# Moving the start of the MLP's operands by 216 bytes within their tiles, in a two-layer encoder on one core

## The chip, the cores and the metric

The kernel runs on one core of a Trainium2 chip. The metric is the device time of one execution in microseconds (us). The kernel before takes 2055.51 us, the median of three runs (2053.45 to 2055.89).

## What is computed

The reference is a two-layer bidirectional encoder in float32, with 256 tokens of width 2048. Each layer adds a token mixer with cross-attention, and then a dense MLP with squared ReLU of width 8192. The change concerns the MLP, so only its part is shown in full:

```python
h = x
for i in range(DEPTH):                       # 2 layers
    n = rms_norm(h, attn_norm[i])
    ...                                      # attention heads, concatenated
    h = h + jnp.concatenate([mix, cross], axis=-1) @ w_o[i]
    n = rms_norm(h, mlp_norm[i])
    h = h + jnp.square(jax.nn.relu(n @ w_up[i])) @ w_down[i]
return rms_norm(h, final_norm)
```

## The kernel before, in words

Every matrix product is done on float32 data split in two parts: ScalarE (ACT) copies a value into the rounded type float32r, the "hi" part (line 303), and VectorE (DVE) subtracts it from the value to leave the "lo" part (line 304). A product is then three matmuls: hi x hi, hi x lo and lo x hi. In a matmul one operand stays in the array (the weights in the trace's sense, loaded by an instruction of its own that the profile shows as PEld) and the other is moved past it.

**The MLP.** Its input, hT, holds the normalised activations by feature: 128 partitions, 16 blocks of 512 columns, the first 256 of a block being the hi part of the 256 tokens and the next 256 the lo part. It is a tile of tag "wide" in the pool "keep", got by `wide` (line 423), which gives 512 bytes of room and takes an offset in bytes, `at`. The attention's input nT uses the same tag at offset 480; hT uses 0 (line 617).

The up weights come in chunks of 128 x 2048, each in one DMA into the tile raw_U (`loaded`). `half_of_side` (line 706) splits half a chunk, 128 x 1024, into two tiles uh and ul, each with 256 bytes of room and two buffers; it has an offset in bytes too, `place`, which is 0 for the up products. Other callers give it MOVING_AT = 160: three chunks of the second layer's input projection that are prepared early (`prep_early`) and the last, plain part of the down product (`plain_grains`), where uh and ul are the moved operand.

`u_products` (line 696) does eight blocks of one half chunk, three matmuls each (lines 702, 703, 704): uh against the hi part of hT, uh against its lo part, and ul against the hi part. In all three the 128 x 128 slice of uh or ul is the weights and 256 columns of hT move. A chunk is 48 such matmuls, and the two layers have 128 chunks, 6144 matmuls in all. The result, ps_u, goes through ReLU and square on ACT (lines 756, 757).

The down product is done by a scheme that saves products: per step a set "first" (bh, bl; three products) and a set "second" (th, tl; four products), three matmuls of 512 columns for each product (lines 816, 817, 818). Here the activations a_s are the weights and the split down weights move. There are 112 such steps, and the last eighth of the hidden width goes through plain products (lines 208, 211, 212).

**Order.** The kernel lists "grains" of work (`add_mlp`): first the up products of the hidden width's first eighth, then alternately half a chunk of up products and one set of the down side, for seven eighths, then the plain part. Each grain has earlier stages for loading and splitting, called a fixed number of grains ahead. A scheduler then sets the order on each engine. On PE it comes out as 48 up matmuls, then 12 on th and tl, then 9 on bh and bl, and so on; in some steps two of the 48 stand ahead of the last down matmuls.

Of the kernel before, what the change touches and what calls it, by code (L numbers as in the profile page):

```python
# [40 lines left out]
GUARD = 3  # L41

MOVING_AT = 160
MASKED = -1e30


# [27 lines left out]
def encoder_kernel(ctx: ExitStack, tc: tile.TileContext, t: dict, out: bass.AP):  # L74
# [4 lines left out]
    def opened(name, side="left", space=None, bufs=1):  # L79
        kw = {"space": space} if space else {}  # L80
        manager = tc.tile_pool(name=name, bufs=bufs, side=side, reuse_waits="tile", **kw)
        pools[name] = manager, manager.__enter__()
        return pools[name][1]

    def closed(*names):
        for name in names:
            pools.pop(name)[0].__exit__(None, None, None)
# [56 lines left out]
    def halves_of(w):  # L144
# [6 lines left out]
        def prep_early(hf):  # L151
            tiles[hf] = half_of_side(tiles["raw"], hf, MOVING_AT)

# [35 lines left out]
    def later(n, fn, *args):  # L189
        pending.append((state["tick"] + n, fn, args))  # L190
# [110 lines left out]
    def split(dst_hi, dst_lo, src):  # L301

        first = nc.scalar.activation(dst_hi, src, AF.Copy)  # L303
        return first, nc.vector.tensor_tensor(dst_lo, src, dst_hi.bitcast(F32), op=ALU.subtract)  # L304
# [10 lines left out]
    def transposed(dst, src, ks, which):  # L315

        for a in range(0, len(ks), 2):
            pt = at.att.tile([P, 2, SEQ], F32, tag="att", name="pt_n")
            for b, k in enumerate(ks[a : a + 2]):
                for i in range(NT):  # L320
                    nc.tensor.transpose(pt[:, b, i * P : (i + 1) * P], src(i, k), ident)  # L321
            for b, k in enumerate(ks[a : a + 2]):
                last = split_pair(dst, pt[:, b, :], which, k)
        return last
# [98 lines left out]
    def wide(name, at=0):  # L423
        room = keep.tile([P, KT * 512 + P], F32R, tag="wide", name=name)
        return room[:, at // 4 : at // 4 + KT * 512].rearrange("p (a b) -> p a b", b=512)
# [164 lines left out]
    def sum_squares(which, i, nb):  # L590
        sq = at.side.tile([P, 512], BF16, tag="junk", bufs=1, name="sq")
        nc.scalar.activation(sq, h[:, i, nb * 512 : (nb + 1) * 512], AF.Square,
                             accum_out=ssq[which][:, i, nb : nb + 1])

    def mean_square(which, n, name):

        s = small.tile([P, NT], F32, tag="ss0", name="ss_t")
        nc.vector.tensor_reduce(s, ssq[which][:, :, :n], axis=AX.X, op=ALU.add)
        v = keep.tile([P, NT], F32, tag=name, name=name)
        nc.vector.tensor_scalar(v, s, 1.0 / (n * 512), EPS, op0=ALU.mult, op1=ALU.add)  # L600
        return v
# [7 lines left out]
    def o_done(layer, nb):  # L609
        which = 2 * layer  # L610

        def guard():

            box["near"] = mean_square(which, GUARD, "near")
            box["scale"] = keep.tile([P, NT], F32, tag="scale", name="scale")
            nc.gpsimd.tensor_tensor(box["scale"], box["near"], mhalf[:, :NT], op=ALU.pow)
            box["hT"] = wide(f"hT{layer}")

        def begun():

            y = at.side.tile([P, NT, 512], F32, tag="T", bufs=2, name="h_s")
            for i in range(NT):
                nc.scalar.activation(y[:, i, :], h[:, i, D - 512 :], AF.Copy, scale=box["scale"][:, i : i + 1])
            box["begun"] = y

        def scaled(b):
            y = at.side.tile([P, NT, 512], F32, tag="T", bufs=2, name="h_s")
            for i in range(NT):
                nc.scalar.activation(y[:, i, :], h[:, i, b * 512 : (b + 1) * 512], AF.Copy,
                                     scale=box["scale"][:, i : i + 1])  # L630
            transposed(box["hT"], lambda i, k: y[:, i, k % 4 * P : (k % 4 + 1) * P],
                       list(range(b * 4, b * 4 + 4)), (G_M0, G_M1)[layer])

        def inv():

            v = mean_square(which, 4, "full")
            box["inv"] = keep.tile([P, NT], F32, tag="inv", name="inv")
            nc.vector.reciprocal(v, v)
            nc.vector.tensor_tensor(box["inv"], v, box["near"], op=ALU.mult)
            box["ninv"] = keep.tile([P, NT], F32, tag="ninv", name="ninv")  # L640
            nc.vector.tensor_scalar(box["ninv"], box["inv"], -1.0, None, op0=ALU.mult)

        def f(w):
            if nb == 0:
                closed("work")
                at.side = opened("side", side="right")
            def add():
                for i in range(NT):
                    hs = h[:, i, nb * 512 : (nb + 1) * 512]
                    nc.vector.tensor_tensor(hs, w.ps[i], hs, op=ALU.add)  # L650

            def squares():
                for i in range(NT):
                    sum_squares(which, i, nb)

            if nb < 3:
                add()
                squares()
            if nb == GUARD - 1:
                later(1, guard)  # L660
                for b in range(GUARD):
                    later(2 + 2 * b, scaled, b)
                later(7, begun)
            if nb == 3:
                y = box["begun"]
                for i in range(NT):
                    nc.vector.scalar_tensor_tensor(y[:, i, :], w.ps[i], box["scale"][:, i : i + 1], y[:, i, :],
                                                   op0=ALU.mult, op1=ALU.add)
                box["ready"] = transposed(box["hT"], lambda i, k: y[:, i, k % 4 * P : (k % 4 + 1) * P],
                                          list(range(12, KT)), (G_M0, G_M1)[layer])  # L670
                later(4, past, add)
                later(6, past, squares)
                later(8, past, inv)
        return f
# [28 lines left out]
            nc.tensor.matmul(ps, hi[:, s], acts[:, k, SEQ:], start=False, stop=False)  # L703
            nc.tensor.matmul(ps, lo[:, s], acts[:, k, :SEQ], start=False, stop=k == KT - 1)  # L704

    def half_of_side(raw, hf, place=0):
        s = slice(place // 4, place // 4 + HALF)
        tiles = tuple(at.side.tile([P, HALF + 64], F32R, tag=n, bufs=2, name=n)[:, s] for n in ("uh", "ul"))
        box.setdefault("splits", []).append(split(*tiles, raw[:, hf * HALF : (hf + 1) * HALF]))
        return tiles  # L710
# [6 lines left out]
    def up_grains(layer, part, m):  # L717
# [5 lines left out]
        def prep(hf):  # L723
            own[hf] = half_of_side(own["raw"], hf)
# [145 lines left out]
    def plain_grains(layer, nb):  # L870
# [9 lines left out]
        def prep(c, hf):  # L880
            if c == 0:
                own[c, hf] = half_of_side(own[0], hf, MOVING_AT)
            else:
                own[c, hf] = tuple(at.mlp.tile([P, HALF], F32R, tag="bt"[hf] + x, name=f"{x}_p") for x in "hl")
                split(*own[c, hf], own[1][:, hf * HALF : (hf + 1) * HALF])
# [273 lines left out]
def expanded_bias(rpb):  # L1159
# [6 lines left out]
    dc = np.clip(cols[None, :] - cols[:, None] + WIN_W - 1, 0, 2 * WIN_W - 2)  # L1166
    res = np.full((nh, 2, GRID_W, BJ, GRID_W), MASKED, np.float32)
    for r in range(2):
        for j in range(BJ):
            dr = j + ROWS + 1 - r  # L1170
            res[:, r, :, j, :] = np.where(inside[None], rpb[:, dr][:, dc], np.float32(MASKED))
    return res.reshape(nh, P, BJ * GRID_W)
# [64 lines left out]
```

## Time and profile before

| | |
|---|---|
| median of three runs | 2055.51 us |
| the profiled execution | 2053.93 us |
| its span, first to last instruction | 2052.1 us |
| granted TensorE clock, mean | 0.999 |
| PE busy | 2029.9 us, 12516 matmuls |
| up products (lines 702, 703, 704), 2048 matmuls each | 568.6, 567.9 and 568.4 us busy, 278 ns each |
| split of uh (ACT, line 303) | 278 of 1061 ns |
| split of ul (DVE, line 304) | 278 of 1219 ns |

Matmuls are pipelined: one of 256 columns is shown with 278 ns, yet the next one starts some 113 ns after it. So for PE the rows' durations and the busy share don't tell the rate; the differences between start times in the timeline do. In the timeline a row gives the start in us from the span's start, the duration in us, engine, line, operation, the tiles (result <- moved operand and weights) and the shapes. A table of stretches gives, for each engine, busy time and in brackets the number of instructions that began there.

### The profile page before, as it was taken

How to read it: one execution, taken by the hardware profiler on the slowest of the kernel's cores; microseconds unless marked ns; L12 is line 12 of the kernel's file. 1: busy time of each engine (PE TensorE's matmuls, PEld its weight loads, DVE VectorE, ACT ScalarE, POOL GpSimd, SP SyncE). 2: the span in 40 equal slices, each digit the busy share in tenths (PEclk: the TensorE clock that was granted, in tenths of full speed). 3: DMA queues.
4: the chain of work that ended last, by engine and by line, in shares of the span. 5: the costliest groups of instructions: out<-in, count | busy, mean ns of one | idle time of the engine just before them, and what ended most of it. 6: DMA issues, size and time to landing. Idle time of an engine off the chain costs nothing.

```text
span 2052.1 us, 31583 instructions
## 1 busy us (share of the span) xinstructions
PE 2029.9 (99%) x12516; PEld 1812.2 (88%) x12516; DVE 1669.2 (81%) x2061; ACT 1252.7 (61%) x1652; POOL 119.3 (6%) x144
## 2 busy tenths in 40 slices
PE   8999999999999999999999999999999999999998
PEld 7888888889999999999988888889999999999996
DVE  6767666558998999989897667657988999999896
ACT  6755555556666666666656557556666666666664
POOL 0000000000000000000000001000000000000000
PEclk9999999999999999999999999999999999999999
DMA  7755555727777777787765554536877787887773
GB/s 280 283 190 179 188 176 171 276 88 223 231 231 231 221 237 230 220 243 224 225 218 205 176 180 144 194 116 221 242 226 231 217 238 221 237 229 224 235 219 135
DMA packets 93429, 433.79 MB, mean 211 GB/s; under 512 B 10464, under 2 KB 12128, under 8 KB 60128
## 3 DMA queue, kind: packets, MB, share of 16 engines
q1 hardware_dynamic: 75888, 399.25, 57.7%
q0 software_dynamic: 16816, 31.46, 8.7%
q8 instruction: 98, 1.61, 0.3%
q10 hardware_dynamic: 576, 1.05, 0.1%
q14 instruction: 51, 0.42, 0.1%
HBM read 398.17 MB, written 4.19 MB: 196 GB/s over the span
## 4 chain that ended last, share of the span: by engine, by line
PE 97%; ACT 1%; DVE 1%; issue 0%; DMA 0%; SPq 0%; POOLq 0%; POOL 0%; ACTq 0%
PE ps_u L704 11%; PE ps_u L702 11%; PE ps_u L703 11%; PE p L816 9%; PE p L817 9%; PE p L818 9%; PE ps_m L208 8%; PE ps_m L211 8%; PE ps_m L212 8%; PE ps_s L221 6%; PE ps_s L224 3%; PE pt_a L384 1%; PE pt_n L321 1%; DMA raw<-in_w_km 0%; PE av L392 0%
## 5 line engine op out<-in xcount | busy, mean ns | idle before, releaser
L704 PE MATMUL ps_u<-hT,ul 128*128 128x256 f32 x2048 | 568.4, 278 | 1.8 <-DVE ul L304 1.8
L702 PE MATMUL ps_u<-hT,uh 128*128 128x256 f32 x2048 | 568.6, 278 | 0.2
L703 PE MATMUL ps_u<-hT,uh 128*128 128x256 f32 x2048 | 567.9, 277 | 0.0
L303 ACT ACTIVATE uh<-raw_U 128x1024 fp32r<-128x1024 f32 x278 | 294.8, 1061 | 315.8 <-PE ps_u L703 294.8
L304 DVE TENSOR_TENSOR lo<-raw,hi 128x1024 fp32r<-128x1024 f32 (+1 forms) x224 | 266.4, 1195 | 161.7 <-ACT hi L303 158.4
L702 PEld LDWEIGHTS ps_u<-hT,uh 128*128 128x128 f32 x2048 | 384.9, 188 | 5.8 <-ACT uh L303 0.6
L704 PEld LDWEIGHTS ps_u<-hT,ul 128*128 128x128 f32 x2048 | 385.9, 189 | 3.7 <-DVE ul L304 2.6
L703 PEld LDWEIGHTS ps_u<-hT,uh 128*128 128x128 f32 x2048 | 384.4, 188 | 4.5
L304 DVE TENSOR_TENSOR ul<-raw_U,uh 128x1024 fp32r<-128x1024 f32 x278 | 337.6, 1219 | 40.5 <-ACT uh L303 40.4
L303 ACT ACTIVATE hi<-raw 128x1024 fp32r<-128x1024 f32 (+1 forms) x224 | 231.7, 1039 | 210.4 <-PE ps_m L212 117.8
L303 ACT ACTIVATE th<-t 128x2048 fp32r<-128x2048 f32 x112 | 215.1, 1920 | 123.5 <-PE p L818 117.1
L304 DVE TENSOR_TENSOR tl<-t,th 128x2048 fp32r<-128x2048 f32 x112 | 256.3, 2288 | 34.5 <-ACT th L303 34.1
L304 DVE TENSOR_TENSOR bl<-b,bh 128x1536 fp32r<-128x1536 f32 x112 | 196.1, 1751 | 0.3 <-ACT bh L303 0.2
L817 PE MATMUL p<-tl,a_s 128*128 128x512 f32 x448 | 177.2, 395 | 0.0
L818 PE MATMUL p<-th,a_s 128*128 128x512 f32 x448 | 174.4, 389 | 0.0
L303 ACT ACTIVATE bh<-b 128x1536 fp32r<-128x1536 f32 x112 | 166.2, 1484 | 10.2 <-PE p L818 4.0
L816 PE MATMUL p<-th,a_s 128*128 128x512 f32 x448 | 166.1, 395 | 0.0
L796 POOL DMA_DIRECT2D t<-b x112 | 97.1, 867 | 1164.5 <-DVE t L795 510.3
L221 PE MATMUL ps_s<-nT,hi 128*128 128x512 f32 x448 | 142.5, 397 | 0.0
L818 PE MATMUL p<-bh,a_s 128*128 128x512 f32 x336 | 131.1, 390 | 0.0
L817 PE MATMUL p<-bl,a_s 128*128 128x512 f32 x336 | 130.9, 390 | 0.0
L795 DVE TENSOR_TENSOR t<-t,b 128x512 f32<-128x512 f32 x112 | 77.2, 689 | 50.8 <-DMA t<-in_w_pair 43.7
(237 smaller groups left out, 3508.2 us busy)
## 6 DMA issues: line engine op xcount, KB each, us to landing
raw_U<-in_w_up SPq DMA_DIRECT2D x128, 1024.0 KB, 6.6
b<-in_w_pair SPq DMA_DIRECT2D x112, 768.0 KB, 4.5
raw<-in_w_o SPq DMA_DIRECT2D x32, 1024.0 KB, 5.0
t<-in_w_pair SPq DMA_DIRECT2D x112, 256.0 KB, 3.4
t<-b POOLq DMA_DIRECT2D x112, 256.0 KB, 6.7
raw<-in_w_b SPq DMA_DIRECT2D x21, 1024.0 KB, 4.9
raw<-in_w_av SPq DMA_DIRECT2D x12, 1024.0 KB, 4.9
raw<-in_w_aq SPq DMA_DIRECT2D x12, 1024.0 KB, 4.9
```

The lines of the kernel that those rows point to most:

```text
L208: first = nc.tensor.matmul(w.ps[i], ah, hi[:, s], start=st, stop=False)
L211: nc.tensor.matmul(w.ps[i], ah, lo[:, s], start=False, stop=False)
L212: nc.tensor.matmul(w.ps[i], al, hi[:, s], start=False, stop=sp)
L221: nc.tensor.matmul(ps, hi[:, s], acts[:, k0 + j, :], start=k0 + j == 0, stop=False)
L303: first = nc.scalar.activation(dst_hi, src, AF.Copy)
L304: return first, nc.vector.tensor_tensor(dst_lo, src, dst_hi.bitcast(F32), op=ALU.subtract)
L702: nc.tensor.matmul(ps, hi[:, s], acts[:, k, :SEQ], start=k == 0, stop=False)
L703: nc.tensor.matmul(ps, hi[:, s], acts[:, k, SEQ:], start=False, stop=False)
L704: nc.tensor.matmul(ps, lo[:, s], acts[:, k, :SEQ], start=False, stop=k == KT - 1)
L816: nc.tensor.matmul(ps, a[:, 0, ai, :], hi[:, s], start=begins, stop=False)
L817: nc.tensor.matmul(ps, a[:, 0, ai, :], lo[:, s], start=False, stop=False)
L818: nc.tensor.matmul(ps, a[:, 1, ai, :], hi[:, s], start=False, stop=ends)
```

## The change

hT begins 216 bytes further on in its tile, and so do uh and ul wherever no other offset is given, that is in the up products. 216 bytes are 54 float32 elements. The tiles keep their sizes and their places, since the room was there already; the calls with MOVING_AT = 160 and nT at 480 stay.

```diff
 MOVING_AT = 160
+UP_AT = 216
 MASKED = -1e30
...
             nc.gpsimd.tensor_tensor(box["scale"], box["near"], mhalf[:, :NT], op=ALU.pow)
-            box["hT"] = wide(f"hT{layer}")
+            box["hT"] = wide(f"hT{layer}", UP_AT)
...
-    def half_of_side(raw, hf, place=0):
+    def half_of_side(raw, hf, place=UP_AT):
         s = slice(place // 4, place // 4 + HALF)
         tiles = tuple(at.side.tile([P, HALF + 64], F32R, tag=n, bufs=2, name=n)[:, s] for n in ("uh", "ul"))
```

## The prediction

> **What bounds the kernel now.** I read the page's busy line first, then the chain that ended last.
>
> ```profile
> PE 2029.9 (99%) x12516; PEld 1812.2 (88%) x12516; DVE 1669.2 (81%) x2061; ACT 1252.7 (61%) x1652; POOL 119.3 (6%) x144
> ...
> PE 97%; ACT 1%; DVE 1%; issue 0%; DMA 0%; SPq 0%; POOLq 0%; POOL 0%; ACTq 0%
> ```
>
> TensorE is busy for 99% of the span and makes up 97% of the chain. So a matmul that starts a nanosecond later after its predecessor moves the end by a nanosecond; nothing else matters much. The table of stretches says the same of one inner eighth of an MLP (eight steps of 10.31 us), and gives two stretches of the eighth's opening, when up products run alone, in layer 0 (from 462 us) and layer 1 (from 1390 us):
>
> ```profile
> core 0: us, PE busy (x) PEld busy (x) DVE busy (x) ACT busy (x) POOL busy (x), PEclk, DMA share, GB/s
> ...
> 584.50:667.00 82.50, 82.50 (x554) 75.47 (x553) 74.56 (x80) 54.54 (x57) 6.98 (x8) 1.00 0.78 231
> 462.00:482.00 20.00, 20.00 (x179) 20.00 (x178) 13.42 (x16) 12.42 (x18) 1.05 (x1) 1.00 0.58 179
> 1390.00:1410.00 20.00, 20.00 (x172) 20.00 (x171) 12.28 (x15) 11.39 (x17) 0.30 (x1) 1.00 0.58 207
> ```
>
> In the eighth PE has no idle time and a granted clock of 1.00; DVE is busy for 74.56 of 82.50 us, so it has a tenth to spare. The other two rows are what everything below rests on: the same products, the same addresses, the same clock, and 179 matmuls against 172 in 20 us. So the rate of a stream of matmuls has at least two values. Since a busy time cannot show this, I went to the timeline of PE and took differences of start times. One regular step (48 up products, then 21 of the down side):
>
> ```profile
> 698.02 0.39 PE L818 MATMUL p<-bh,a_s 128*128 128x512 f32 x1
> 698.25 0.28 PE L702 MATMUL ps_u<-hT,uh 128*128 128x256 f32 x1
> 698.37 0.28 PE L703 MATMUL ps_u<-hT,uh 128*128 128x256 f32 x1
> 698.49 0.28 PE L704 MATMUL ps_u<-hT,ul 128*128 128x256 f32 x1
> 698.61 0.29 PE L702 MATMUL ps_u<-hT,uh 128*128 128x256 f32 x1
> ...
> 703.50 0.28 PE L703 MATMUL ps_u<-hT,uh 128*128 128x256 f32 x1
> 703.61 0.28 PE L704 MATMUL ps_u<-hT,ul 128*128 128x256 f32 x1
> 703.73 0.40 PE L816 MATMUL p<-th,a_s 128*128 128x512 f32 x1
> ```
>
> The first five gaps are 118, 120, 119, 123, 118 ns; then it settles at 113.3 until the end: 48 products take 5.48 us. The step after it begins otherwise, two up products being put ahead of the last downs:
>
> ```profile
> 707.19 0.28 PE L702 MATMUL ps_u<-hT,uh 128*128 128x256 f32 x1
> 707.31 0.28 PE L703 MATMUL ps_u<-hT,uh 128*128 128x256 f32 x1
> 707.43 0.39 PE L817 MATMUL p<-bl,a_s 128*128 128x512 f32 x1
> ...
> 708.82 0.28 PE L704 MATMUL ps_u<-hT,ul 128*128 128x256 f32 x1
> 708.93 0.28 PE L702 MATMUL ps_u<-hT,uh 128*128 128x256 f32 x1
> ...
> 714.23 0.39 PE L816 MATMUL p<-th,a_s 128*128 128x512 f32 x1
> ```
>
> Here 46 products take 5.41 us, 117.7 ns each, and never settle. Such steps recur once an eighth, always slow. The down products (512 columns) settle at 226.7 ns, twice 113.3, but their first twelve after an up block (those on th and tl) are slow too: 693.43 to 698.25 us holds 21 of them, 4.82 us instead of 4.76. Over the whole trace the gaps stand above these two floors by 8.0 us in the up products (1562 of 6144 gaps are over 115 ns; 22 real stalls apart), by 6.2 us in th/tl and 0.9 us in bh/bl. **15 us is all that the kernel can win while the floors hold.**
>
> **The change, part by part.** It adds and removes no instruction; in the two built programs every engine has the same instructions in the same order (source lines from 44 on are one higher), and every tile has the same address. What moves is where in its tile an operand begins. hT's tile starts at byte 34464 of its partition, uh's at 199648 and 204000, ul's at 208352 and 212704, all multiples of 32. With 216 added all begin 8 bytes past a multiple of 16. Moving operand (hT) and weights (uh, ul) move together, so their distance stays.
>
> 1. *Splits into uh, ul and hT (ACT, DVE).* 256 of the 278 rows of 1061 (ACT) and 1219 ns (DVE) serve the up products. Begun at multiples of 64 (hi, lo) the same operations take 1063 and 1223 ns, so alignment from 32 to 64 changes nothing; 8 past 16 isn't in the trace. Taken at 0, between no gain (both engines are off the chain) and a loss that begins only at some 500 ns more for each: the cover is DVE's idle 7.94 us in an eighth, which holds 16 such splits. With that gone DVE would be the bound.
> 2. *DMAs.* None touches the moved operands; raw_U stays. 0.
> 3. *The settled rate of up products.* 113.3 ns with both operands 32 past 64; down products with both at multiples of 64 run at exactly twice that for twice the columns. Between these two the start makes no difference. I take 0. Bounds: 117.8 above, the other settled rate; below, nothing in the trace runs 256 columns under 113.3 at length, which leaves a small chance.
> 4. *How each block settles.* A weight load starts 3 ns after the previous matmul and runs beside it; in the slow mode that of ul takes 192 ns instead of 188 and matmuls 281 instead of 276. So the two streams disturb each other, and which mode they fall into is decided at the entry, while one side still reads the down side's addresses (all multiples of 64) and the other the up side's. That distance does change, by 216 bytes, and so all entries are drawn anew. The trace has eleven entries of other kinds besides the regular one: after interruptions between 444 and 486 us and between 1376 and 1418 us (six that settle with an excess of 5 to 15 ns in all, two that stay at 117.8), the first regular step of a layer (8 ns), the start of the MLP (33 ns, like the regular one) and the split step (never). The regular entry, 33 ns, is one of the dear ones; 7 of 11 are cheaper by about 22 ns. Likewise th's entry costs 55 ns, where blocks of 512 columns elsewhere (products on nT after attention or after other products) pay 41, 23 and 0, mean 21.
>
> The likeliest draw gives: 98 regular blocks x 22 ns = 2.2 us; 13 split steps' worth of blocks x 46 x 4.4 ns, less 10 each = 2.5, times 7 in 11 = 1.6; layer 1's slow opening, 264 x 4.4 ns = 1.2, times 7 in 11 = 0.7; 112 th blocks x 34 ns = 3.8. **Sum 8.3 us.** The profiled execution took 2053.93 us (span 2052.1 and 1.8 around it), giving 2045.6; the median of the runs shown is 1.6 above that execution, so 2047.2 beside it.
>
> **A rule of the Trainium skill.** "SBUF — State Buffer", Specifications, gives SBUF 16-byte lines, each crossing to a new one paying a penalty. By it the new start would be worse; no matmul operand of the trace begins off a 16-byte line, so it neither agrees nor disagrees. What it would do is a rival below.
>
> **Rivals.**
> - *Nothing happens* (20%): addresses play no part in the entries, which are a matter of instruction timing. For it: DVE's and ACT's work leaves no mark on the gaps. Then 2055.5.
> - *The regular entry falls into the slow mode* (20%). Slower. For it: three of eleven entries do. Price: 96 blocks x (48 x 4.4 - 33) = 17.1 us, and with it 1.6 us for layer 0's opening (361 x 4.4 ns): 2074. It decides once more than some 47 of the 96 blocks fall there, for that eats the 8.3.
> - *One more piece is read per operand* (12%): 256 columns of 4 bytes are 64 pieces of 16 bytes from a multiple of 16, and 65 from 8 past it; if pieces are what is paid, 113.3 / 64 = 1.8 ns x 6144 = 10.9 us: 2066. Against it: 32 past 64 and 0 past 64 cost the same, so no coarser piece is paid. This is the line rule of the Trainium skill, priced here from rows.
> - *The floor itself moves* (3% down by several ns, below 2040; 3% up beyond 117.8, above 2080).
>
> **How the numbers follow.** Forecast 42%, at 2047. Faster by over 0.2% (4 us; about what a measurement of this kernel can tell from no change): 42 + 3 = 45%; within: 20%; slower: 20 + 12 + 3 = 35%. The forecast's own range is 2041 (all 15 us) to 2051. The range for 8 in 10 goes from 2041 to 2077, over the slow mode's 2074; it leaves out the moved floors and the tails.
>
> **What would show it.** In the after profile the order and counts are as before, and ACT and DVE rows stay within 1%. Right: 48 up products in about 5.45 us and 21 downs in 4.77 to 4.80. Nothing: the same 5.48 and 4.82. Slow mode: 48 in 5.65, with load rows of ul at 192 ns. One more piece: settled gaps of 115, in every block alike. The forecast is wrong if the settled gap moves at all, or if DVE's idle time in an eighth vanishes.

## The result, and the profile after

The changed kernel takes 2090.94 us, the median of four runs (2090.5 to 2091.94), where the kernel before takes 2054.48 (2053.03 to 2055.89). The ratio is 1.0178, with a 95% interval of 1.0166 to 1.019: 36 us slower. The profiled execution took 2090.5 us, with a span of 2088.7.

The page's busy line and its chain by engine:

```profile
PE 2067.5 (99%) x12516; PEld 1850.1 (89%) x12516; DVE 1676.8 (80%) x2061; ACT 1252.2 (60%) x1652; POOL 119.3 (6%) x144
...
PE 98%; ACT 1%; DMA 0%; issue 0%; DVE 0%; SPq 0%; POOLq 0%; POOL 0%; ACTq 0%
```

The counts are those of before, and PE still is the chain. PE's busy time has grown by 37.6 us, about as much as the span (36.6), so the time was not lost in waits. In the page's costliest groups (a line number is one higher than before) the two splits have not moved, and the up products have:

```profile
L703 PE MATMUL ps_u<-hT,uh 128*128 128x256 f32 x2048 | 581.4, 284 | 0.0
...
L304 ACT ACTIVATE uh<-raw_U 128x1024 fp32r<-128x1024 f32 x278 | 295.2, 1063 | 364.0 <-PE ps_u L704 348.5
...
L705 PEld LDWEIGHTS ps_u<-hT,ul 128*128 128x128 f32 x2048 | 389.0, 190 | 2.7 <-DVE ul L305 1.9
L305 DVE TENSOR_TENSOR ul<-raw_U,uh 128x1024 fp32r<-128x1024 f32 x278 | 338.4, 1221 | 50.1 <-ACT uh L304 48.7
```

ACT's split takes 1063 ns (1061 before), DVE's 1221 (1219). An up matmul is shown with 284 ns instead of 278, but as before the durations overlap and only the starts tell the rate. The timeline of PE over one regular block of 48 up products:

```profile
695.76 0.28 PE L703 MATMUL ps_u<-hT,uh 128*128 128x256 f32 x1
695.88 0.28 PE L704 MATMUL ps_u<-hT,uh 128*128 128x256 f32 x1
696.01 0.28 PE L705 MATMUL ps_u<-hT,ul 128*128 128x256 f32 x1
...
701.33 0.28 PE L704 MATMUL ps_u<-hT,uh 128*128 128x256 f32 x1
701.45 0.28 PE L705 MATMUL ps_u<-hT,ul 128*128 128x256 f32 x1
701.57 0.39 PE L817 MATMUL p<-th,a_s 128*128 128x512 f32 x1
```

From 695.76 to 701.57 us are 5.80 us by the trace's full stamps, 120.9 ns for each product, where the block of before took 5.48. And it does not settle: the gaps go on in a pattern of 120 with a 124 or 127 among them, to the end. The table of stretches shows the same rate in both layers' openings, where up products run alone:

```profile
core 0: us, PE busy (x) PEld busy (x) DVE busy (x) ACT busy (x) POOL busy (x), PEclk, DMA share, GB/s
...
463.00:483.00 20.00, 20.00 (x168) 20.00 (x167) 12.50 (x15) 11.70 (x16) 1.05 (x1) 1.00 0.54 175
1405.00:1425.00 20.00, 20.00 (x168) 20.00 (x167) 12.25 (x17) 11.87 (x17) 0.00 (x0) 1.00 0.55 190
```

168 matmuls in 20 us, against 179 and 172 before, at a granted clock of 1.00 all the same. The two modes of before (113.3 and 117.8 ns) are both gone: blocks and openings alike run at about 121 ns (120.4 to 121.1 in the mean of a block).

Summed over the trace, the gaps (from one matmul's start to the next one's) after up products come to 747.8 us (711.1 before), after th and tl products to 310.0 (310.9), after bh and bl products to 230.5 (229.6). That is 36.7 - 0.9 + 0.9 = 36.7 us; the two profiled executions differ by 36.6. **All of the loss is in the rate of the 6144 up products.**

### The profile page after: what moved, and what is told of

Its sections match the earlier page's. It is cut to its first block, busy times and chain, and to the rows that moved or that the text cites. A ratio compares the mean times of both kernels' runs of the same rounds, so it can differ in the third digit from the quotient of the medians.

```text
span 2088.7 us, 31583 instructions
## 1 busy us (share of the span) xinstructions
PE 2067.5 (99%) x12516; PEld 1850.1 (89%) x12516; DVE 1676.8 (80%) x2061; ACT 1252.2 (60%) x1652; POOL 119.3 (6%) x144
## 4 chain that ended last, share of the span: by engine, by line
PE 98%; ACT 1%; DMA 0%; issue 0%; DVE 0%; SPq 0%; POOLq 0%; POOL 0%; ACTq 0%
PE ps_u L703 12%; PE ps_u L704 12%; PE ps_u L705 12%; PE p L817 9%; PE p L819 9%; PE p L818 9%; PE ps_m L209 8%; PE ps_m L212 8%; PE ps_m L213 8%; PE ps_s L222 6%; PE ps_s L225 3%; PE pt_a L385 1%; PE pt_n L322 1%; DMA raw<-in_w_km 0%; PE av L393 0%
## 5 line engine op out<-in xcount | busy, mean ns | idle before, releaser
L703 PE MATMUL ps_u<-hT,uh 128*128 128x256 f32 x2048 | 581.4, 284 | 0.0
L705 PE MATMUL ps_u<-hT,ul 128*128 128x256 f32 x2048 | 578.8, 283 | 1.5 <-DVE ul L305 1.5
L704 PE MATMUL ps_u<-hT,uh 128*128 128x256 f32 x2048 | 579.6, 283 | 0.0
L304 ACT ACTIVATE uh<-raw_U 128x1024 fp32r<-128x1024 f32 x278 | 295.2, 1063 | 364.0 <-PE ps_u L704 348.5
L305 DVE TENSOR_TENSOR ul<-raw_U,uh 128x1024 fp32r<-128x1024 f32 x278 | 338.4, 1221 | 50.1 <-ACT uh L304 48.7
L304 ACT ACTIVATE hi<-raw 128x1024 fp32r<-128x1024 f32 (+1 forms) x224 | 231.7, 1039 | 210.3 <-PE ps_m L213 117.8
L819 PE MATMUL p<-bh,a_s 128*128 128x512 f32 x336 | 131.9, 393 | 0.0
L817 PE MATMUL p<-bh,a_s 128*128 128x512 f32 x336 | 108.4, 390 | 2.1 <-ACT c L757 2.1
```

The costliest lines, as they stand in the source:

```text
L703: nc.tensor.matmul(ps, hi[:, s], acts[:, k, :SEQ], start=k == 0, stop=False)
L817: nc.tensor.matmul(ps, a[:, 0, ai, :], hi[:, s], start=begins, stop=False)
L819: nc.tensor.matmul(ps, a[:, 1, ai, :], hi[:, s], start=False, stop=ends)
```

## The experiments

The theory after the result, called L: a matmul with an operand that begins off a 16-byte line of its partition (at an address that is no multiple of 16) cannot run at 113.3 ns. Its rivals: only one of the two operands matters (M the moved one, W the weights); or the distance between streams counts, and not the start itself (D, the idea of the prediction's step 4). In the edits below the base is the kernel before. Most are single runs, each beside the kernel before on the same chip. Fifteen runs of the kernel before on one chip spread from 2052.6 to 2057.6 us, so a single time tells nothing of a difference of a few us; there the sums of gaps must speak.

**Each operand alone, and neighbours of 216 on a line.**

```diff
# e1_input_only
-            box["hT"] = wide(f"hT{layer}")
+            box["hT"] = wide(f"hT{layer}", 216)
# e2_weights_only
-    def half_of_side(raw, hf, place=0):
+    def half_of_side(raw, hf, place=216):
# e3_both_224: both edits with 224.  e4_both_208: both with 208
```

> hT alone begins 216 bytes further on, the weights stay. Theory M (a moved operand that begins off a 16-byte line is streamed more slowly): the settled gap of the up products is 120.9 ns as in the changed kernel and the time about 2091 us. Theory W (the weight load is what suffers): settled gap 113.3, about 2055. Theory D (only the distance between the two streams counts): here it changes by 216, so something other than both, any value from 2047 to 2110. If each operand pays its share: between 2060 and 2085.

> uh and ul alone begin 216 bytes further on, hT stays. Theory M: settled gap 113.3 ns, about 2055 us. Theory W: 120.9 and about 2091. Theory D: changed from both, as the distance changes by -216. Shares: this and the run with hT alone add up to 36 us.

> Both move by 224 bytes, 8 more than in the change, so that every operand begins at a multiple of 64. Theories M and W, with a 16-byte or 32-byte line as the unit: settled gap 113.3, 2055 us, or up to 15 us less or 20 us more from the entries into the blocks. Theory D, and any theory in which the distance moved is what counts: like the change, about 2091.

> Both move by 208 bytes, 8 less than in the change: every operand begins at a multiple of 16 that is no multiple of 32. If the unit is a 16-byte line: settled gap 113.3 and about 2055 us (2045 to 2075 with the entries). If the unit is 32 bytes: settled gap above 118 and 2080 or more.

They took 2084.05, 2087.72, 2067.14 and 2049.99 us, beside 2054.16. A regular block's first up product and the first down product behind it, on PE's timeline, for hT alone:

```profile
694.76 0.28 PE L702 MATMUL ps_u<-hT,uh 128*128 128x256 f32 x1
...
700.56 0.39 PE L816 MATMUL p<-th,a_s 128*128 128x512 f32 x1
```

and for the weights alone:

```profile
694.86 0.28 PE L702 MATMUL ps_u<-hT,uh 128*128 128x256 f32 x1
...
700.69 0.40 PE L816 MATMUL p<-th,a_s 128*128 128x512 f32 x1
```

5.80 and 5.83 us: either operand alone brings the block to where both bring it. So M and W both fall, and the two prices do not add up (either alone costs about the whole). The two kernels end a little earlier than the change mainly because th and tl products settle at once behind their blocks (305.1 and 305.7 us in sum instead of 310). With 224 and with 208, 8 bytes to either side of 216, the same two places are

```profile
691.32 0.28 PE L702 MATMUL ps_u<-hT,uh 128*128 128x256 f32 x1
...
696.97 0.40 PE L816 MATMUL p<-th,a_s 128*128 128x512 f32 x1
```

5.65 us, 117.7 ns each, with 224, and with 208

```profile
687.57 0.28 PE L702 MATMUL ps_u<-hT,uh 128*128 128x256 f32 x1
...
693.04 0.39 PE L816 MATMUL p<-th,a_s 128*128 128x512 f32 x1
```

5.47 us. Both are on a line, and both show the modes of the kernel before and nothing else: 224 puts the regular blocks into the slow one, 208 into the fast one. That 224 has not become slow as such shows in its opening, where the same operands run at the full rate:

```profile
465.00:485.00 20.00, 20.00 (x179) 20.00 (x178) 14.28 (x19) 12.54 (x18) 1.05 (x1) 1.00 0.70 223
```

208 is a multiple of 16 and not of 32, so the line is not longer than 16 bytes; runs below with 4, 8 and 12 bytes show that it is not shorter. The moves by 208 and 224 also speak against D: a distance near 216 is not what costs 120.9.

**Small moves, the place within 16 bytes, and other matmuls.**

```diff
# e5_both_8, e6_both_32, e8_both_220, e9_both_4, e13_both_12: both edits above with 8, 32, 220, 4, 12
# e7_others_8: hT, and uh and ul of the up products, as before
-MOVING_AT = 160
+MOVING_AT = 168
...
-            box["nT"] = wide("nT0", 480)
+            box["nT"] = wide("nT0", 488)
...
-                box["nT"] = wide("nT1", 480)
+                box["nT"] = wide("nT1", 488)
```

> Both operands move by 8 bytes alone. Theory L (a matmul whose moved operand or weights begin off a 16-byte line can't settle at 113.3 ns; the distance moved does not count): settled gap 120 to 122 ns and 2080 to 2095 us. Theory D (the distance of 216 bytes to the down side's operands is what counts): 8 bytes are a small shift, so near 113.3 ns and 2045 to 2075 us.

> Both move by 32 bytes, to multiples of 64. Theory L: on a line, so one of the two modes, 113.3 or 117.8 ns settled, 2045 to 2072 us. If a start at a multiple of 64 is what makes the up products fall into the 117.8 mode (as with 224 bytes): 117.8 and 2067. If the mode is a matter of how the block is entered: either.

> hT, and uh and ul in the up products, stay as before; nT begins at 488 instead of 480, and the tiles uh and ul that are the moved operand of 512 columns (last part of the down product, and three early chunks) at 168 instead of 160. Theory L: it holds for other matmuls as well: 192 products on a_p and 72 on nT with uh or ul moved go from 227 to about 240 ns, products on nT as weights (hi, lo moved) slow by several ns each, and S products with nT moved from 233 and 116.5 to about 241 and 121; in all 5 to 20 us. If only 256-column streams with a load for each suffer (the load and the stream being nearly of one length): 512-column gaps stay at 227 and the time within 5 us of before.

> Both move by 220 bytes: 12 past a multiple of 16, 4 more than in the change. Theory L with the 16-byte line as the only unit: as the change, settled 120 to 122 ns, 2085 to 2095 us. If pieces of 8 bytes count too: slower than the change, 2095 to 2140.

e5 took 2089.01 us, e6 2064.24, e7 2061.88 and e8 2069.72, beside 2054.15. Eight bytes alone do it: in e5 the opening shows the change's rate,

```profile
465.00:485.00 20.00, 20.00 (x168) 20.00 (x167) 13.51 (x16) 11.31 (x16) 1.05 (x1) 1.00 0.62 207
```

and the mean gap over all up products is 120.7 ns. D is dead for the main effect. e6, at multiples of 64 like 224, has the regular blocks in the slow mode again. Its openings run in the fast one almost throughout, and so do its split steps (113.6 ns), which are slow in the kernel before and with 224 (117.7 and 117.8). e8 missed: 12 past a line cost less than 8 past, 117.7 ns, and in every stretch.

e7 shows that the rule is not one of the up products, which here stay at 711.1 us in sum. The products on a_p are those of the plain part of the down product, with a_p as weights and uh or ul moved, 512 columns each. The first and the seventh of them in a stretch, before

```profile
2003.72 0.39 PE L208 MATMUL ps_m<-uh,a_p 128*128 128x512 f32 x1
...
2005.08 0.39 PE L208 MATMUL ps_m<-h_p,a_p 128*128 128x512 f32 x1
```

and in e7

```profile
2009.64 0.39 PE L208 MATMUL ps_m<-uh,a_p 128*128 128x512 f32 x1
...
2011.03 0.39 PE L208 MATMUL ps_m<-uh,a_p 128*128 128x512 f32 x1
```

Six products take 1.36 us before and 1.39 here. Over all 192 of them, with the moved operand 8 past a line, the median goes from 227 to 235 ns and the mean up by 7 (about 240 was expected). With the weights (nT) off a line and 512 columns moved, 227 becomes 230; 72 products with nT as weights and uh or ul moved, both off a line, go to 231. In S products (lines 221 and 224), where nT is moved, the 256-column gaps go from 116.5 to 120.4 in the mean and the 512-column ones from 234.7 to 235.2. So the price did not double with twice the columns: 7 to 8 ns at 512 on a_p, 7.5 at 256 in the up products. It does not grow with the number of 16-byte pieces; but it is not one price for all matmuls either, as the 0.5, 3 and 4 ns of the others show.

> Both operands move by 4 bytes, to 4 past a multiple of 16; 8 past gave a settled gap of 120.8 ns, 12 past 117.7. Theory L1 (a fixed cost per matmul for the 16-byte pieces that are cut at both ends, whatever the cut): 120 to 122 ns and 2085 to 2091 us; the 117.7 at 12 past would then be the slow mode of operands on a line, seen by chance. Theory L2 (the place within the 16 bytes counts, 12 and 4 alike as odd fours): 117 to 118.5 ns and 2065 to 2075 us.

> Both operands move by 12 bytes, the same place within 16 bytes as 220 but another distance and another remainder by 64 (44 instead of 60). If the place within the 16 bytes sets the cost: settled 117.5 to 118 ns in every stretch and 2066 to 2073 us. If 117.7 at 220 was a matter of its distance: about 120.9 and 2082 to 2091.

e9 took 2084.34 us, beside 2053.77, with gaps of 121.0 in the mean, and e13 took 2068.25, beside 2053.53, with 117.8. Their openings:

```profile
465.00:485.00 20.00, 20.00 (x167) 20.00 (x166) 13.83 (x16) 11.25 (x16) 1.05 (x1) 1.00 0.67 212
```

for 4 bytes, and for 12 bytes

```profile
465.00:485.00 20.00, 20.00 (x172) 20.00 (x172) 13.11 (x15) 11.66 (x16) 1.05 (x1) 1.00 0.66 202
```

So the place within 16 bytes sets the price: 4 and 8 past cost 7.5 ns or a little more, 12 past 4.4, at 12 as at 220. L1 fell for 12 past, and L2 fell for 4 past. The 117.7 at 12 past is near the slow mode's 117.8, yet another thing: it goes 117, 117, 119, has the second matmul of three as its dearest (118.9 in the mean), and stands in every stretch, openings included.

**Other starts on a line, and a version that beats both.**

```diff
# e10_both_16, e11_both_240: both edits with 16, 240.  e12_208_timed: e4's kernel
# e14_240_nT496: both with 240, and nT0 and nT1 at 496.  e15_240_nT464: nT at 464
```

> Both move by 16 bytes, 48 past a multiple of 64 as with 208. On a 16-byte line, so settled at 113.3 or 117.8 ns. If the start's remainder by 64 picks the mode of the regular block: 113.3 as with 208, 2045 to 2056 us. If the full distance to the down side's operands picks it: 117.8 is as likely, 2062 to 2070.

> Both move by 240 bytes, to 16 past a multiple of 64, a remainder not tried yet. On a line: settled at 113.3 or 117.8 ns, so 2045 to 2056 or 2062 to 2070 us, and nothing near the 120.8 of 216. A gap of 120 or more would say that the line is of 32 bytes after all.

> The kernel with 208 bytes, which ended at 2049.99 us in one look, timed against the kernel before. Its up products settle at 113.3 ns in every eighth but start some 9 ns dearer per block; its trace holds 2.9 us less in the up products and about 1 us less on the down side. If that is its doing: ratio 0.997 to 0.999. If it was chance of one run: 1.000.

> Both moved by 240, and nT from 480 to 496, so that all three begin 16 past a multiple of 64. The up products as with 240 alone: 2050. If starts at 16 past 64 also help where nT is moved (S products, 233 and 116.5 ns, floors 226.7 and 113.3), up to 4 us more: 2046 to 2050, ratio 0.996 to 0.9985. If the S products' excess comes from the alternation of 512 and 256 columns: no further gain.

> Both moved by 240, and nT at 464, 48 past a multiple of 64. As with nT at 496: 2046 to 2050 us if the start of nT counts in the S products, 2050 if their alternation of widths sets the excess.

16 and 240 bytes took 2051.44 and 2049.82 us, beside 2053.77. 208, run eleven times, took 2050.57 in the median, a ratio of 0.9985 with an interval of 0.9976 to 0.9994. So there is a better start than either kernel's, by about 3 us. In all three no stretch of up products runs at 117.8 any more. A regular block with 240 takes 5.46 us, where it took 5.48 before:

```profile
688.23 0.28 PE L702 MATMUL ps_u<-hT,uh 128*128 128x256 f32 x1
...
693.69 0.40 PE L816 MATMUL p<-th,a_s 128*128 128x512 f32 x1
```

With nT moved as well nothing more came, and most of the gain went: 2052.48 us, ratio 0.9996 (0.9987 to 1.0005), and 2051.78. In e14 the up and down products' gaps are those of 240 alone, but products with nT as weights go from a median of 227 to 232 and 233 ns, nearly 3 us in all, and the S products gain 0.9 us at 512 columns and lose as much at 256. nT at 496 is on a line too, and it cost these products more than 8 past a line did in e7 (230 ns). So a start on a line is not cheap for every product, and the start that suits the up products does not suit these.

All the moves of hT, uh and ul, with the sums of gaps in us. The mean leaves out the 16 to 23 gaps of over 140 ns, which are stalls; the sums hold all gaps. The last column but one adds up the three differences from before. The last is the measured difference in time: for 216 of the two profiled executions, for the others of the single run from the kernel before on its chip (208 timed: -3.2).

| start moved by | past 16 / past 64 | mean up gap, ns | up | th, tl | bh, bl | sum of differences | measured |
|---|---|---|---|---|---|---|---|
| 0 (before) | 0 / 32 | 114.6 | 711.1 | 310.9 | 229.6 | | |
| 216 (change) | 8 / 56 | 120.9 | 747.8 | 310.0 | 230.5 | 36.7 | 36.6 |
| hT alone 216 | 8 / 56 | 120.7 | 747.0 | 305.1 | 229.4 | 29.9 | 29.9 |
| uh, ul alone 216 | 8 / 56 | 121.1 | 749.8 | 305.7 | 230.1 | 34.0 | 33.6 |
| 8 | 8 / 40 | 120.7 | 747.1 | 310.0 | 229.8 | 35.3 | 34.9 |
| 4 | 4 / 36 | 121.0 | 748.6 | 305.2 | 228.8 | 31.0 | 30.6 |
| 12 | 12 / 44 | 117.8 | 729.8 | 306.1 | 229.1 | 13.4 | 14.7 |
| 220 | 12 / 60 | 117.7 | 729.2 | 307.4 | 230.0 | 15.0 | 15.6 |
| 32 | 0 / 0 | 117.1 | 726.2 | 306.1 | 229.8 | 10.5 | 10.1 |
| 224 | 0 / 0 | 117.2 | 727.4 | 307.6 | 229.2 | 12.6 | 13.0 |
| 16 | 0 / 48 | 113.9 | 706.9 | 312.1 | 230.0 | -2.6 | -2.3 |
| 208 | 0 / 48 | 114.1 | 708.2 | 309.4 | 230.1 | -3.9 | -4.2 |
| 240 | 0 / 16 | 113.8 | 706.4 | 310.2 | 230.3 | -4.7 | -4.0 |

## Why the prediction was wrong

- *What bounds the kernel* was right: every difference in the table is one of PE's gaps, to within 1.3 us, and what the up products lost per matmul came out at the end 6144 times.
- *Step 1* (splits) and *step 2* (DMAs) were right: 1063 and 1221 ns, and no transfer in the chain.
- **Step 3 failed**, and with it the forecast: "Between these two the start makes no difference. I take 0", with 117.8 ns as the upper bound. The settled gap went to 120.9. The step took two starts, 0 and 32 past 64, and inferred from them to a start of another kind, off a 16-byte line, which by the prediction's own words no matmul operand of the trace has. It took the worst rate seen for a bound as well; but that rate belonged to operands on a line and bounds nothing for one that is off it. The range's upper end, 2077, came from that bound.
- *Step 4* was right about what it described and wrong about where it applies. On a line there are two modes, the entry decides between them, and another start draws the entries anew: to longer times (32, 224) or shorter ones (16, 208, 240). Its sum was mis-sized too, 8.3 us forecast and 2 to 4 got: the split steps and layer 1's opening did become fast, but the regular entry stayed dear (21 to 36 ns over the floor, 33 before) and th's entry too (309 to 312 us in sum, 311 before). At 216 there is only one rate, and no draw.
- *"Moving operand (hT) and weights (uh, ul) move together, so their distance stays"* was true and beside the point: each operand's own start costs, alone, as much as both.
- *The rival with one more piece* named the right condition, a start off a 16-byte line, with 12%, and the wrong size: 1.8 ns per product forecast, 7.5 over the floor measured (6.2 in the mean, since before was not always on the floor). It took one piece to cost a 64th of the gap; what a start off the line costs is about four times that, and depends on the place within the line, which one more piece does not explain.
- *The floor itself moves, "3% up beyond 117.8, above 2080"*, is the rival that came true: 120.9 ns and 2091 us. It stood without a mechanism or a sum, and its case lay outside the range.
- *The slow-mode rival* did not happen in the change, but it is what 224 bytes give: 2067 measured where 2074 was worked out for a slow regular entry. The difference is mainly that th's blocks became cheaper by 3.3 us and that layer 0's opening stayed fast.

What stays open: why a start off the line costs a matmul 0.5 to 8 ns and not one fixed price, why 12 past is cheaper than 4 and 8 past, and why one operand off its line costs as much as two. The trace shows when instructions start, not what the streams fetch. Which entry leads to which mode on a line is open too. In the regular blocks a remainder by 64 of 0 went with the slow mode twice, and 16, 32 and 48 with the fast one four times. But at 0 past 64 the split steps were fast with 32 bytes and slow with 224, so the remainder alone does not decide.

The Trainium skill ("SBUF — State Buffer", Specifications) says that SBUF has 16-byte lines and that each crossing to a new one pays a penalty. The runs agree on the 16 bytes (208, 16 and 240 are multiples of 16 and not of 32, and are not slower) and that leaving them costs; no run here tells whether a crossing is what is paid. By the prediction's count a start off the line adds one line at either width (64 become 65, 128 become 129), which goes with the like price on a_p at 512 columns; but it adds one at 12 past as well, where 4.4 ns are paid and not 7.5, and with both operands off it adds two, which cost no more than one.

## What to carry to other kernels

Let both operands of a matmul begin at a multiple of 16 bytes in their partition; where PE is the bound, a start off that grid cost the up products 3 to 8 ns for every matmul (other products 0.5 to 8), which no busy share shows, so take differences of start times. On the grid, try two or three starts for each operand by itself: the same products settled at 113.3 or 117.8 ns by how a block was entered, and 16 bytes more, good for hT, cost the products on nT 5 to 6 ns. And when a change takes an operand to a kind of address that the trace does not hold, the rates of the trace are no bound: leave the range open on that side.

## What was not expected of the hardware

- One operand off its line is as bad as two: 120.7 and 121.1 ns alone, 120.9 together.
- Down products behind a block with hT alone at 216 settle at once (227.0 ns in the mean for th and tl, against 231.3 before). With 4 bytes and with the weights alone they do so too (227.1 and 227.4), with 8 and with the change, at the same up rate, they don't (230.7 in both); no run shows why.
- A 12-byte remainder costs 4.4 ns where 4 and 8 cost 7.5.
